# One backbone layer on one core: a gated unit's weights are split in the first loop, its sums lie in three freed banks, and the attention's preparation gets an order

## The chip, the core and the metric

The kernel runs on one core of one Trainium2 chip. The metric is the device time of one execution, in microseconds (us); less is better. The core has five engines that each work through their own list of instructions in order: PE (matrix products into the accumulation banks), DVE, ACT and POOL (elementwise work), and SP (which here only issues transfers). An instruction waits for its inputs, and everything behind it on the same engine waits with it.

## What is computed

One layer of a backbone: an input is normed and modulated, one wide projection feeds three mixers, and the mixers are merged. Only the first part matters here. `h` is the modulated image (1024 tokens by 1024 channels), `hc` the modulated context (256 tokens):

```python
def hybrid_layer(x, xc, c, c_ctx, lp, update_ctx):
    h, gate = modulate(x, c, lp['norm_g'], lp['w_ada'], lp['b_ada'])
    hc, gate_c = modulate(xc, c_ctx, lp['norm_g'], lp['w_ada'], lp['b_ada'])
    z = h @ lp['w_in']
    kc, vc = na_kv(hc @ lp['w_in'][:, A_K:A_Z], lp['k_norm_g'])
    q = na_query(z, lp['q_norm_g'])
    k, v = na_kv(z[..., A_K:A_Z], lp['k_norm_g'])
    ya = neighbourhood_attention(q, k, v, kc, vc, lp['rpb']) * jax.nn.silu(z[..., A_Z:B_B])
    yb = short_conv_branch(z, lp['conv_short_w'])
    yc = conformer_branch(z, lp['conv_conf_w'], lp['conv_conf_b'], lp['ln_conf_g'], lp['ln_conf_b'])
    return x + gate * merge_branches(z, ya, yb, yc, ...)

def conformer_branch(z, w_conv, b_conv, ln_g, ln_b):
    a, g = z[..., C_GLU:C_GLU + D_BRANCH], z[..., C_GLU + D_BRANCH:C_Z]
    u = dw_conv(a * jax.nn.sigmoid(g), w_conv) + b_conv
    ...
```

The "gated unit" is `a * sigmoid(g)`. Its 512 channels are made in four parts of 128, and the first of them (`glu_steps(0, ...)`) is the one the change touches.

## The kernel before

Every product of two numbers in full precision is made of three products of rounded ones: a tensor is split into a high part (a rounded copy) and a low part (the rest), and PE sums high by high, high by low and low by high (`mm3`, lines L107 to L109). So each weight or activation costs a cast (mostly ACT) and a subtraction (DVE or POOL) before PE may use it.

Up to the attention the program does the following.

1. **First loop** (`for k in range(KT)`, eight channel blocks). For each k, `image_ada` makes the modulation of block k on DVE (results A_t, B_t), `modulated` turns four token tiles of x on PE (tile xT_ps), ACT writes the high part `ha` and the full value `xh`, DVE subtracts for the low part (L353). `outer(k, ...)` then adds block k into the query/key/value sums of those four token tiles, all open at once in banks (`first`). `second(k - LAG)` does the same for token tiles 4 and 5 (tiles `hb`), three blocks later. `ctx_ada` (L382, tile `junk`), on DVE, makes the context's modulation out of the same weights: 16 instructions of 1024 columns.
2. **Rest of the image.** `rest_image` modulates token tiles 6 and 7, and `qkv(0, ...)` sums their query/key/value from the finished `h` (L107 to L109, tile ps).
3. **`middle`.** It runs three pieces: first half of the gated unit (weights CGL, sums in tile gps), `context_h` (modulation of the context: tiles `ch`, split with DVE for xh and POOL for the low part), second half of the gated unit (weights CA, sums aps).
4. **Context sums** (`context`, tile psc), then the next head pair's weights (`w1`), then the attention of head pair 0 (`attend(0)`): masks and biases on POOL (L497, L541), `stacks` (copies and splits of q, k, v for one head, L516 to L524), scores (sl, sc), exponent on ACT (L568), and so on. While the attention runs, PE is filled up with the projections of later parts.

Where instructions stand is decided when the program is built: the framework plays the program through on a timeline of its own and gives each engine a fixed list from that. A line moved in the source therefore moves instructions of other lines too. `tc.issue_after(x)` keeps what stands under it behind instruction x in that play, without changing what is computed.

Two pools matter. Banks: there are eight; ps_m has two (tag m), ps_q one (tag q), and pst has tag t (two, for xT_ps) and tag k (three). In the first loop six open sums take m, m, k, k, k, q. Before, both halves of the gated unit take their banks from ps_m, and the context sums take two of the three k banks. Working tiles: rows of 1024 columns (`row4k`, 15 of them) hold x, the ada weights and, before, both weight halves of the gated unit (ghi, glo). The tag `cht` (four tiles) is for the context tiles of later head pairs, which are first loaded in `qkv(1)`.

Of the kernel before, what the change touches and what calls it, by code (L numbers as in the profile page):

```python
# [45 lines left out]
def tile_hybrid(ctx: ExitStack, tc, x, xT, cx, cond, crow, ng, w_ada, b_ada, wqkv, wz,  # L46
# [82 lines left out]

    def qkv(hp, w=None, cts=None, first=(), psc=None, mid=None):  # L130
        w = w or qkv_weights(hp)
# [40 lines left out]
        def context():  # L172
# [3 lines left out]
            vc = [a1.tile([P, 2, P], F32R, tag=f"vc{h}", name="vc") for h in range(2)]  # L176
            pc = psc or [ps_m.tile([P, 512], F32, tag="m", name="psc"), ps_q.tile([P, 512], F32, tag="q", name="psc")]
            for k in range(KT):
# [79 lines left out]

    def glu(i, load=None):
        for _ in glu_steps(i, load):  # L260
            pass

    def glu_steps(i, load=None):
        sg = []
        load = load or (lambda src: load_w(src, KT, pool))
        w = load(wz[CGL + i])
        for b in range(2):
            ps = ps_m.tile([P, 512], F32, tag="m", name="gps")
            mm3(ps, [(w[k][0], w[k][1], hcols(0, k, B512[b]), hcols(1, k, B512[b])) for k in range(KT)])
            t = tmp("flt")  # L270
            act.activation(t, ps, AF.Tanh, scale=0.5)
            sg.append(t)
        yield
        w = load(wz[CA + i])
        for b in range(2):
            ps = ps_m.tile([P, 512], F32, tag="m", name="aps")
            mm3(ps, [(w[k][0], w[k][1], hcols(0, k, B512[b]), hcols(1, k, B512[b])) for k in range(KT)])
            dve.scalar_tensor_tensor(out=sg[b], in0=sg[b], scalar=1.0, in1=ps, op0=ALU.add, op1=ALU.mult)
            nc.sync.dma_start(ud[i][:, B512[b]], sg[b])

    with tc.tile_pool(name="st", bufs=1) as st, tc.tile_pool(name="ps_t", bufs=1, space=PSUM) as pst:
# [107 lines left out]
        def outer(k, ts):  # L389
            for t in ts:  # L390
# [12 lines left out]
        for k in range(KT):  # L403
# [42 lines left out]

        def load_rows(src):
            hi, lo = row4k("ghi", F32R), row4k("glo", F32R)
            for o in range(0, D, 384):
                sl = slice(o, min(o + 384, D))  # L450
                raw = wp.tile([P, 384], F32, tag="wr", name="wr", bufs=3)
                n = sl.stop - o
                state["rows"] = nc.sync.dma_start(raw[:, :n], src[:, sl])
                act.copy(hi[:, sl], raw[:, :n])
                dve.tensor_tensor(out=lo[:, sl], in0=raw[:, :n], in1=hi[:, sl].bitcast(F32), op=ALU.subtract)
            return [(hi[:, k * P : k * P + P], lo[:, k * P : k * P + P]) for k in range(KT)]

        def context_h():
# [7 lines left out]
        def middle():  # L466
            g = glu_steps(0, load_rows)
            for c in (0, 1, 0):
                context_h() if c else next(g, None)
            with tc.issue_after(state["rows"].ins):  # L470
                eight_columns()

        w1raw = []
        for k in range(0, RAW1, 2):
            r = row4k("w1raw")
            nc.sync.dma_start(r[:, :768], wqkv[1, :, k * 384 : k * 384 + 768])
            w1raw += [r[:, :384], r[:, 384:768]]
        qkv(0, w0, ch0, first, [pst.tile([P, 512], F32, tag="k", name="psc", bufs=3) for _ in range(2)], middle)

# [4 lines left out]
    with tc.tile_pool(name="at", bufs=1, reuse_waits="tile") as at, \  # L484
# [10 lines left out]
        for h in range(2):  # L495
            t = at.tile([P, SPAN + 512], F32, name=f"bias{h}")
            pool.memset(t, 1e30)  # L497
            biases.append(t)
        qlz = []
        for h in range(2):  # L500
            t = at.tile([P, QB, P], F32R, name=f"qlz{h}")
            pool.memset(t[HD - h * HD : P - h * HD].bitcast(F32), 0.0)
            qlz.append(t)
# [44 lines left out]
        def scores(b0, qd, ql, ks, kc, bias):  # L548
# [8 lines left out]
            for i in range(2):  # L557
# [9 lines left out]
                dve.tensor_tensor_reduce(pl, sl[:, :n], bias[:, o : o + n], 1.0, mn[:, i : i + 1], ALU.add, ALU.min, mn[:, 2 + i : 3 + i])  # L567
                act.activation(pc, sc[:, i], AF.Exp, bias=mn[:, 2 + i : 3 + i], scale=-1.0, accum_out=mn[:, 4 + i : 5 + i])  # L568
                act.activation(pl, pl, AF.Exp, bias=mn[:, 2 + i : 3 + i], scale=-1.0, accum_out=mn[:, 6 + i : 7 + i])
                pts.append((pt, n))  # L570
            dve.tensor_tensor(out=mn[:, 0:2], in0=mn[:, 4:6], in1=mn[:, 6:8], op=ALU.add)
            dve.reciprocal(out=mn[:, 0:2], in_=mn[:, 0:2])
# [13 lines left out]
        def attend(hp):  # L586
            ya = at.tile([P, 16, 64], F32, tag="ya", name="ya", bufs=1)
            for h in range(2):
                bias = bias_of(2 * hp + h)
                qd, ql, ks, kc, vs, vc = stacks(hp, h)  # L590
                hs = slice(h * HD, h * HD + HD)
# [821 lines left out]
```

## Time and profile before

| | us |
|---|---|
| median of 3 runs (lowest to highest) | 1121.64 (1121.34 to 1122.14) |
| the profiled execution, its own time | 1122.98 |
| its span, first to last instruction | 1121.2 |

| engine | busy us | share of the span |
|---|---|---|
| ACT | 519.8 | 46% |
| POOL | 653.8 | 58% |

An engine's share is a mean over stages that have different limits. Matmuls overlap: a matmul's shown duration is longer than the time to the next one's start, so a count of matmuls times the step between starts tells more than busy time. PEclk is the clock granted to PE, in tenths of full speed. In a timeline row the columns are start (us from the span's start), duration, engine, source line, operation, written tile and read tiles, sizes, count; in square brackets the idle time before it and what ended it.

### The profile page before, as it was taken

Reading aid. Unit: us, or ns where it says so; the run is one execution under the profiler, and the core shown is the slowest. Engines: PE = TensorE matmul, PEld = TensorE weight load, DVE = VectorE, ACT = ScalarE, POOL = GpSimd, SP = SyncE. Lnnn points to the kernel's source line nnn. Section 1 sums busy time; section 2 is a strip of 40 time slices with the busy share of each in tenths; the row PEclk is TensorE's granted clock in tenths of the full one; section 3 lists DMA queues with packets and bytes.
Section 4 is the critical chain, followed back from the end, with each engine's and each line's share of the span. In section 5 each row is a group of like instructions: output and inputs, shape, how many; then the busy total and the mean of one; then the engine's idle time right before and its main releaser. Section 6 shows DMA issues by size and latency. Waiting matters only on the chain. (4 is left out here: it accounts for less than half of the span.)

```text
span 1121.2 us, 15882 instructions
## 1 busy us (share of the span) xinstructions
PE 1084.2 (97%) x5330; PEld 923.2 (82%) x5330; DVE 832.6 (74%) x1368; ACT 519.8 (46%) x1108; POOL 653.8 (58%) x643
## 2 busy tenths in 40 slices
PE   6889999999999999999999999999999999999998
PEld 5768898998998888887888888888888788878766
DVE  6983478666765655557995997897992479879995
ACT  6764576567556554445233232323434434533430
POOL 2254957437636951104958586868777562783860
PEclk7999999999999999999999999999999999999999
DMA  9555414313312332218133424343436996462443
GB/s 351 203 190 190 122 44 120 94 57 93 118 54 85 122 120 70 67 49 326 38 132 104 151 85 160 103 153 139 129 134 237 408 327 222 140 215 66 126 155 122
DMA packets 79458, 163.17 MB, mean 146 GB/s; under 512 B 10289, under 2 KB 31153, under 8 KB 79281
## 3 DMA queue, kind: packets, MB, share of 16 engines
q1 hardware_dynamic: 74768, 160.06, 41.5%
q10 hardware_dynamic: 4608, 2.10, 0.6%
q8 instruction: 42, 0.69, 0.3%
q14 instruction: 40, 0.32, 0.1%
HBM read 120.18 MB, written 44.50 MB: 147 GB/s over the span
## 5 line engine op out<-in xcount | busy, mean ns | idle before, releaser
L751 DVE SCALAR_TENSOR_TENSOR cv<-upad,cf_t,cv 128x512 f32<-128x512 f32 x240 | 166.8, 744 | 0.1
L699 POOL TENSOR_TENSOR wl<-s,wh 128x512 fp32r<-128x512 f32 x69 | 98.4, 1439 | 21.8 <-ACT wh L698 8.1
L90 POOL TENSOR_TENSOR wl<-wr,wh 128x384 fp32r<-128x384 f32 (+1 forms) x57 | 57.3, 1012 | 68.2 <-ACT wh L88 57.6
L698 ACT CAST wh<-s 128x512 fp32r<-128x512 f32 x92 | 55.9, 616 | 87.6 <-POOL s L702 66.0
L584 DVE TENSOR_TENSOR plo<-pp,phi 128x256 fp32r<-128x256 f32 (+2 forms) x96 | 54.5, 576 | 34.8 <-ACT phi L583 34.4
L541 POOL TENSOR_TENSOR bias<-mk,img 64x96 f32<-64x96 bf16 (+1 forms) x96 | 43.7, 462 | 36.9 <-DVE mn L567 20.5
L699 POOL TENSOR_TENSOR wl<-wr,wh 128x512 fp32r<-128x512 f32 x44 | 60.5, 1375 | 4.2 <-ACT wh L698 4.2
L775 PE MATMUL ga<-ha,wh 128*128 128x512 f32 x152 | 59.3, 390 | 1.2 <-ACT wh L698 1.2
L777 PE MATMUL ga<-ha,wl 128*128 128x512 f32 x152 | 59.2, 390 | 0.0
L776 PE MATMUL ga<-ha,wh 128*128 128x512 f32 x152 | 59.2, 390 | 0.0
L583 ACT CAST phi<-pp 128x256 fp32r<-128x256 f32 (+2 forms) x96 | 46.5, 494 | 26.6 <-PE pp L581 25.9
L567 DVE CUSTOM_DVE_ANT_0 pt<-sl,bias,mn 128x384 f32<-128x384 f32 (+1 forms) x64 | 37.2, 581 | 23.0 <-PE sl L564 21.7
L88 ACT CAST wh<-wr 128x384 fp32r<-128x384 f32 (+1 forms) x66 | 31.6, 487 | 39.8 <-PE zaps L108 14.3
L568 ACT ACTIVATE pt<-sc,mn 128x256 f32<-128x256 f32 x64 | 30.4, 475 | 40.1 <-DVE mn L567 40.0
L581 PE MATMUL pp<-ident,pt 128*128 128x128 f32 x304 | 47.0, 273 | 1.6 <-DVE pt L574 1.6
L803 POOL TENSOR_TENSOR s<-wr 128x512 f32<-128x512 f32 x16 | 23.8, 1486 | 38.7 <-DMA wr<-in_wz 38.6
L581 PEld LDWEIGHTS pp<-ident,pt 128*128 128x128 f32 x304 | 37.4, 140 | 9.0 <-ACT phi L583 1.3
L79 POOL TENSOR_TENSOR ssh<-ssh,half_neg 128x4 f32<-128x4 f32 (+1 forms) x40 | 41.4, 1036 | 2.9
L574 DVE TENSOR_SCALAR pt<-pt,mn 128x640 f32<-128x640 f32 (+1 forms) x64 | 41.6, 692 | 0.9
L78 POOL TENSOR_SCALAR ssh<-ssh 128x4 f32<-128x4 f32 (+1 forms) x40 | 10.5, 261 | 53.1 <-DVE ssh L227 49.4
L964 ACT ACTIVATE c<-c 128x512 f32<-128x512 f32 x18 | 11.4, 633 | 63.6 <-DVE c L781 48.0
L109 PE MATMUL ps<-wh,hb 128*128 128x384 f32 x112 | 39.3, 354 | 1.2 <-DVE hb L353 1.1
(421 smaller groups left out, 3896.8 us busy)
## 6 DMA issues: line engine op xcount, KB each, us to landing
wr<-in_wz SPq DMA_DIRECT2D x34, 512.0 KB, 4.0
gs<-gd SPq DMA_DIRECT2D x24, 512.0 KB, 5.0
wada<-in_w_ada SPq DMA_DIRECT2D x16, 512.0 KB, 8.7
wrf<-in_wo SPq DMA_DIRECT2D x16, 512.0 KB, 3.6
wr<-in_wz SPq DMA_DIRECT2D x36, 192.0 KB, 2.4
cht<-chd SPq DMA_DIRECT2D x24, 256.0 KB, 3.1
wro<-in_wout SPq DMA_DIRECT2D x24, 256.0 KB, 5.2
gd<-gate SPq DMA_DIRECT2D x22, 256.0 KB, 4.2
```

Of the source, the lines that this page charges most:

```text
L90: lo_eng.tensor_tensor(out=lo[:, :n], in0=raw[:, :n], in1=hi[:, :n].bitcast(F32), op=ALU.subtract)
L541: pool.tensor_tensor(out=dst, in0=mv, in1=iv, op=ALU.subtract)
L574: dve.tensor_scalar(out=pt[:, SPAN - n :], in0=pt[:, SPAN - n :], scalar1=mn[:, i : i + 1], scalar2=0.5, op0=ALU.mult, op1=ALU.mult)
L581: pe.transpose(out=pp[:, c * P : c * P + P], in_=src, identity=ident)
L583: act.copy(hi, v)
L584: dve.tensor_tensor(out=lo, in0=v, in1=hi.bitcast(F32), op=ALU.subtract)
L698: act.copy(hi, src)
L699: eng.tensor_tensor(out=lo, in0=src, in1=hi.bitcast(F32), op=ALU.subtract)
L751: dve.scalar_tensor_tensor(out=acc[b], in0=src, scalar=cf_t[:, i, j : j + 1], in1=acc[b], op0=ALU.mult, op1=ALU.add)
L775: pe.matmul(ps, wh, bh, start=first and j == 0, stop=False, skip_group_check=True)
L776: pe.matmul(ps, wh, bl, start=False, stop=False, skip_group_check=True)
L777: pe.matmul(ps, wl, bh, start=False, stop=last and j == 3, skip_group_check=True)
```

## The change

Three things change.

- **Weights of the first half.** `load_rows(wz[CGL])` is now called in the first loop, at k = 6 (`GATED`). It splits the 1024 columns in four pieces of 256 (before: 384, 384, 256), into four tiles `grow` of the tag `cht`. The second half (CA) is split as before, in rows, but in pieces of 256.
- **Banks.** The sums gps and aps now use the three banks of tag k, as the image sums that held them are copied out. The context sums go to one bank of ps_m and the bank of ps_q.
- **Order of the attention's preparation.** The four memsets for bias and qlz wait for the last `pow` of the context keys' norm (`state["kc"][0]`). The `stacks` of the second head of pair 0 wait for the first exponent (`state["exp"]`).

```diff
+GATED = 6
-    def qkv(hp, w=None, cts=None, first=(), psc=None, mid=None):
+    def qkv(hp, w=None, cts=None, first=(), mid=None):
...
-            pc = psc or [ps_m.tile([P, 512], F32, tag="m", name="psc"), ps_q.tile([P, 512], F32, tag="q", name="psc")]
+            pc = [ps_m.tile([P, 512], F32, tag="m", name="psc"), ps_q.tile([P, 512], F32, tag="q", name="psc")]
...
-    def glu_steps(i, load=None):
+    def glu_steps(i, load, bank):
...
-            ps = ps_m.tile([P, 512], F32, tag="m", name="gps")
+            ps = bank("gps")
...
-            ps = ps_m.tile([P, 512], F32, tag="m", name="aps")
+            ps = bank("aps")
...
+        gated = []
+
+        def load_rows(src, quarters=None):
+            if quarters:
+                hi, lo = ([t[:, i] for t in quarters[2 * n : 2 * n + 2] for i in range(2)] for n in range(2))
+            else:
+                hi, lo = ([t[:, o : o + 256] for o in range(0, D, 256)] for t in (row4k("ghi", F32R), row4k("glo", F32R)))
+            for o in range(4):
+                raw = wp.tile([P, 384], F32, tag="wr", name="wr", bufs=3)
+                state["rows"] = nc.sync.dma_start(raw[:, :256], src[:, o * 256 : o * 256 + 256])
+                act.copy(hi[o], raw[:, :256])
+                dve.tensor_tensor(out=lo[o], in0=raw[:, :256], in1=hi[o].bitcast(F32), op=ALU.subtract)
...
+            if k == GATED:
+                gated.append(load_rows(wz[CGL], [a1.tile([P, 2, 256], F32R, tag="cht", name="grow", bufs=4) for _ in range(4)]))
...
         def middle():
-            g = glu_steps(0, load_rows)
+            g = glu_steps(0, lambda src: gated.pop() if gated else load_rows(src), lambda name: pst.tile([P, 512], F32, tag="k", name=name, bufs=3))
...
-        qkv(0, w0, ch0, first, [pst.tile([P, 512], F32, tag="k", name="psc", bufs=3) for _ in range(2)], middle)
+        qkv(0, w0, ch0, first, middle)
...
-            pool.memset(t, 1e30)
+            with tc.issue_after(state["kc"][0].ins):
+                pool.memset(t, 1e30)
...
-            pool.memset(t[HD - h * HD : P - h * HD].bitcast(F32), 0.0)
+            with tc.issue_after(state["kc"][0].ins):
+                pool.memset(t[HD - h * HD : P - h * HD].bitcast(F32), 0.0)
...
+            state.setdefault("exp", e)
...
-                qd, ql, ks, kc, vs, vc = stacks(hp, h)
+                with tc.issue_after(state["exp"].ins) if hp == 0 and h else ExitStack():
+                    qd, ql, ks, kc, vs, vc = stacks(hp, h)
```

What this makes of the fixed lists is shown at three places. Most source lines count one more after the change (L107 becomes L108), and buffer numbers differ between the two programs.

PE, end of the first loop, before: tiles hb with a number are channel blocks of the image (669, 683 and 697 are blocks 5, 6 and 7), xT_ps is a turned tile.

```order
L394 MATMUL ps<-wh,hb_641 128x384 x2
L392 MATMUL ps<-wh,hb_669 128x384
L393 MATMUL ps<-wl,hb_669 128x384
L392 MATMUL ps<-wh,hb_669 128x384
L393 MATMUL ps<-wl,hb_669 128x384
L394 MATMUL ps<-wh,hb_669 128x384 x2
L392 MATMUL ps<-wh,hb_683 128x384
L393 MATMUL ps<-wl,hb_683 128x384
L392 MATMUL ps<-wh,hb_683 128x384
L393 MATMUL ps<-wl,hb_683 128x384
L345 MATMUL xT_ps<-ident,xt 128x128 x4
L394 MATMUL ps<-wh,hb_683 128x384 x2
```

PE at the same place now (689 and 703 are blocks 5 and 6); these rows are the end of a run of 20 matmuls gps.

```order
L108 MATMUL gps<-ha_170,grow 128x512
L109 MATMUL gps<-ha_170,grow 128x512
L110 MATMUL gps<-ha_170,grow 128x512
L108 MATMUL gps<-ha_171,grow 128x512
L109 MATMUL gps<-ha_171,grow 128x512
L394 MATMUL ps<-wh,hb_689 128x384 x2
L392 MATMUL ps<-wh,hb_703 128x384
L393 MATMUL ps<-wl,hb_703 128x384
L392 MATMUL ps<-wh,hb_703 128x384
L393 MATMUL ps<-wl,hb_703 128x384
L345 MATMUL xT_ps<-ident,xt 128x128 x3
L394 MATMUL ps<-wh,hb_703 128x384 x2
```

Before, the 48 matmuls gps stood in one run behind all of the image's sums; now 20 stand inside the first loop's last blocks, 4 before the sums of token tiles 6 and 7, and 24 between those.

POOL, from the last context tile to the first bias, before: ch is a context tile, wl the low part of the next pair's weights, ssh the norm's sum of squares, vc the context values.

```order
L353 TENSOR_TENSOR ch_1099<-xh,ch_1099 128x256
L90 TENSOR_TENSOR wl<-wr,wh 128x384
L497 MEMSET bias_1334 128x896
L497 MEMSET bias_1336 128x896
L502 MEMSET qlz_1338 64x1024
L502 MEMSET qlz_1340 64x1024
L78 TENSOR_SCALAR ssh<-ssh 128x2
L90 TENSOR_TENSOR wl<-wr,wh 128x384
L78 TENSOR_SCALAR ssh<-ssh 128x2
L79 TENSOR_TENSOR ssh<-ssh,half_neg 128x2 x2
L209 TENSOR_TENSOR vc<-rawc,vc 128x64 x4
L541 TENSOR_TENSOR bias_1334<-mk,img 64x3x48
```

POOL at the same place now.

```order
L79 TENSOR_SCALAR ssh<-ssh 128x2
L80 TENSOR_TENSOR ssh<-ssh,half_neg 128x2
L91 TENSOR_TENSOR wl<-w1raw,wh 128x384 x3
L91 TENSOR_TENSOR wl<-wr,wh 128x384
L79 TENSOR_SCALAR ssh<-ssh 128x2
L80 TENSOR_TENSOR ssh<-ssh,half_neg 128x2
L210 TENSOR_TENSOR vc<-rawc,vc 128x64 x4
L503 MEMSET bias_1344 128x896
L503 MEMSET bias_1346 128x896
L509 MEMSET qlz_1348 64x1024
L509 MEMSET qlz_1350 64x1024
L548 TENSOR_TENSOR bias_1344<-mk,img 64x3x48
```

The memsets went behind the context values, and three subtractions wl, which before stood between the context tiles, went behind the first norm of the context keys.

SP, the transfers of the same stretch, before: wr is a piece of a weight row, mkd and rpd are the mask and the bias table on their way into another layout, vb is v read back, chd the context tile written out.

```order
L325 DMA xt<-in_cx 128x1024 x2
L476 DMA w1raw<-in_wqkv 128x768 x3
L453 DMA wr<-in_wz 128x384 x2
L453 DMA wr<-in_wz 128x256
L249 DMA mkd<-in_mask 16x2x7680
L250 DMA rpd<-in_rpbs 64x6144
L169 DMA vb<-vd_87 128x1x128 x3
L463 DMA chd<-ch_1051 128x2x512
```

SP at the same place now.

```order
L481 DMA w1raw<-in_wqkv 128x768 x3
L468 DMA chd<-ch_1055 128x2x512
L170 DMA vb<-vd_87 128x1x128 x3
L468 DMA chd<-ch_1071 128x2x512
L170 DMA vb<-vd_87 128x1x128
L405 DMA wr<-in_wz 128x256
L468 DMA chd<-ch_1087 128x2x512
L250 DMA mkd<-in_mask 16x2x7680
L251 DMA rpd<-in_rpbs 64x6144
```

The mask and the bias table now leave behind three of the four context tiles and behind the last weight piece of the second half, which needs a buffer that the first piece frees.

More of the change, by code (lines that the diff above doesn't have):

```diff
@@ L257, in tile_hybrid, with glu @@
     B_t = cst.tile([P, KT, 2], F32, name="B_t")
-    def glu(i, load=None):
-        for _ in glu_steps(i, load):
+    def glu(i):
+        for _ in glu_steps(i, lambda src: load_w(src, KT, pool), lambda name: ps_m.tile([P, 512], F32, tag="m", name=name)):
             pass
-    def glu_steps(i, load=None):
+    def glu_steps(i, load, bank):
         sg = []
-        load = load or (lambda src: load_w(src, KT, pool))
         w = load(wz[CGL + i])
         for b in range(2):
-            ps = ps_m.tile([P, 512], F32, tag="m", name="gps")
+            ps = bank("gps")
             mm3(ps, [(w[k][0], w[k][1], hcols(0, k, B512[b]), hcols(1, k, B512[b])) for k in range(KT)])
@@ L394, in outer @@
                 pe.matmul(o, hcols(1, k, sl), w0[k][0], start=False, stop=k == KT - 1)
+        gated = []
[9 more added lines that the diff above has]
+                dve.tensor_tensor(out=lo[o], in0=raw[:, :256], in1=hi[o].bitcast(F32), op=ALU.subtract)
+            return [(hi[k // 2][:, k % 2 * P : k % 2 * P + P], lo[k // 2][:, k % 2 * P : k % 2 * P + P]) for k in range(KT)]
         hlf.append([])
@@ L445, in tile_hybrid @@
         ch0 = []
[L447 to L456, printed above, removed]
         def context_h():
@@ L567, in scores @@
                 dve.tensor_tensor_reduce(pl, sl[:, :n], bias[:, o : o + n], 1.0, mn[:, i : i + 1], ALU.add, ALU.min, mn[:, 2 + i : 3 + i])
-                act.activation(pc, sc[:, i], AF.Exp, bias=mn[:, 2 + i : 3 + i], scale=-1.0, accum_out=mn[:, 4 + i : 5 + i])
+                e = act.activation(pc, sc[:, i], AF.Exp, bias=mn[:, 2 + i : 3 + i], scale=-1.0, accum_out=mn[:, 4 + i : 5 + i])
                 act.activation(pl, pl, AF.Exp, bias=mn[:, 2 + i : 3 + i], scale=-1.0, accum_out=mn[:, 6 + i : 7 + i])
                 pts.append((pt, n))
+            state.setdefault("exp", e)
             dve.tensor_tensor(out=mn[:, 0:2], in0=mn[:, 4:6], in1=mn[:, 6:8], op=ALU.add)
```

## Prediction

> **What bounds the kernel now.** I read the page first, then stretches of ten microseconds, then the timelines of PE and DVE.
>
> ```profile
> span 1121.2 us, 15882 instructions
> ...
> PE 1084.2 (97%) x5330; PEld 923.2 (82%) x5330; DVE 832.6 (74%) x1368; ACT 519.8 (46%) x1108; POOL 653.8 (58%) x643
> ```
>
> PE is busy for 97% of the span, so a change can save only where PE stands idle or crawls. The stretches show where (PE, its weight loads, DVE, ACT, POOL, each busy us and count; then granted clock, DMA share, GB/s).
>
> ```profile
> 30.00:40.00 10.00, 8.00 (x47) 7.09 (x47) 10.00 (x21) 5.57 (x10) 0.00 (x0) 1.00 1.03 392
> ...
> 60.00:70.00 10.00, 7.13 (x36) 5.06 (x36) 10.00 (x24) 9.10 (x21) 5.54 (x7) 1.00 0.52 154
> 70.00:80.00 10.00, 8.94 (x44) 7.98 (x44) 8.38 (x19) 3.75 (x8) 3.86 (x8) 0.83 0.62 222
> 80.00:90.00 10.00, 10.00 (x46) 8.18 (x45) 2.48 (x6) 2.40 (x5) 3.98 (x6) 1.00 0.45 133
> ...
> 110.00:120.00 10.00, 8.47 (x50) 8.08 (x48) 5.25 (x8) 9.86 (x20) 9.56 (x14) 1.00 0.29 85
> ```
>
> From 30 to 78 DVE has almost no free time and PE waits for it: only 36 matmuls run from 60 to 70. From 80 to 90 it is the reverse: PE is full with the first gated half while DVE works 2.48 of 10. The change lays the second stretch over the first.
>
> How much is lost there? The rows below give the steps between matmul starts, and the ends of two stretches.
>
> ```profile
> 55.38 0.33 PE L392 MATMUL ps<-wh,hb 128*128 128x384 f32 x1
> ...
> 81.12 0.39 PE L107 MATMUL gps<-ha,ghi 128*128 128x512 f32 x1
> ...
> 81.80 0.39 PE L107 MATMUL gps<-ha,ghi 128*128 128x512 f32 x1
> ...
> 90.25 0.60 PE L345 MATMUL xT_ps<-ident,xt 128*128 128x128 f32 x4
> 90.61 0.36 PE L188 MATMUL psc<-wh,ch 128*128 128x256 f32 x1
> ...
> 108.08 0.28 PE L190 MATMUL psc<-wh,ch 128*128 128x256 f32 x1
> ...
> 109.16 0.28 PE L190 MATMUL psc<-wh,ch 128*128 128x256 f32 x1
> 109.28 0.34 PE L107 MATMUL ps<-wh,ha 128*128 128x384 f32 x1
> ...
> 112.92 0.51 PE L107 MATMUL ps<-wh,ha 128*128 128x384 f32 x2
> ...
> 118.58 0.33 PE L198 MATMUL pskc<-ident,tmc 128*128 128x128 f32 x1 [0.44 <-DVE tmc L229]
> 120.00 0.45 PE L107 MATMUL ps<-wh,ha 128*128 128x384 f32 x1 [1.09 <-ACT raw L147]
> ```
>
> A 512-wide matmul steps 0.227 (three in 0.68), a 384-wide one 0.173 (21 in 3.64), a 256-wide one 0.12 (nine in 1.08), a turning one 0.09 (four in 0.36). From 55.38 to 109.28, 53.9 us, the list holds 66 of 384 (11.4), 96 of 512 (21.8), 48 of 256 (5.8) and 48 turns (4.3): 43.3 of work, **10.6 lost**. From 109.28 to 120.00, 10.7 us, it holds 48 of 384, two of 256 and two turns, 8.7: **2.0 lost**, nearly all in the two idle times in brackets. So 12.6 us are there to be had.
>
> Part of the first loss is clock, not idleness:
>
> ```profile
> 71.00:72.00 1.00, 1.00 (x4) 1.00 (x4) 1.00 (x5) 0.34 (x1) 0.28 (x1) 0.50 0.89 344
> ```
>
> After the gaps of 60 to 70 PE ran at half clock. [...]
>
> **The change part by part.**
>
> *Weights split in the first loop.* DVE's rows give the prices.
>
> ```profile
> 65.42 1.35 DVE L455 TENSOR_TENSOR glo<-wr,ghi 128x384 fp32r<-128x384 f32 x3
> ...
> 71.55 0.75 DVE L353 TENSOR_TENSOR hb<-xh,hb 128x256 fp32r<-128x256 f32 x2
> 72.22 0.41 DVE L229 TENSOR_TENSOR tm<-raw,ssh 128x256 f32<-128x256 f32 x1
> ...
> 74.55 0.54 DVE L352 TENSOR_SCALAR xh<-xT_ps,A_t,B_t 128x256 f32<-128x256 f32 x1 [0.44 <-ACT hb L347]
> 75.01 0.41 DVE L229 TENSOR_TENSOR tm<-raw,ssh 128x256 f32<-128x256 f32 x1
> 75.34 1.22 DVE L382 SCALAR_TENSOR_TENSOR junk<-wada,sc 128x1024 bf16<-128x1024 f32 x1
> 76.49 0.42 DVE L353 TENSOR_TENSOR hb<-xh,hb 128x256 fp32r<-128x256 f32 x1
> ...
> 96.41 2.44 DVE L455 TENSOR_TENSOR glo<-wr,ghi 128x384 fp32r<-128x384 f32 x3
> ```
>
> Three pieces took DVE 1.27 (65.42 to the next start). Four of 256 cost 0.335 each, as the two hb at 71.55 do: 1.34. They now stand before DVE's parts for blocks 5 to 7, so PE's stretch starts **1.3 later**. The bounds are 0 (another wait covers them) and 2.4 (the same three pieces beside a busy POOL, at 96.41); I take 1.3, since POOL is idle from 30 to 40. [...]
>
> ACT's four casts lie in its free 4.4 us of 30 to 40; without that cover, 1.3. Three transfers of 128 KB go ahead of the last two ada tiles: at 392 GB/s these come 1.0 later, ahead of DVE's backlog still; without that, 1.0.
>
> *Sums of the first half among the image's.* DVE's last part for token tiles 6 and 7 started at 76.49. Its new list puts ahead of it one more junk (1.24), one more xh (0.46), one more tm (0.34) and 0.07 for the pieces: 78.6, ready at 79.0. PE, starting at 56.7, has 64 of 384, 46 of 512 and about 32 turns before it needs that: 24.4, so it comes at 81.1. DVE is then 2 ahead at the end, where it was behind, and the 10.6 shrink to what is still waited for on the way. Block by block the two lists run within half a microsecond of each other; eight blocks, of which some must miss: **1.0**, bounds 0 and 4.
>
> *What is late next.* The context tiles. ACT now copies two image sums and makes a tanh between them, then come the casts of the second half's weights, and PE's aps wait for the first of these. The list brings PE there at 85.1 without waits (69 of 384, 48 of 512, 14 of 256, 43 turns from 56.7). I put the cost at **1.5**, which is three copies of about 0.5 on ACT, bounds 0 and 6 (the first rival). The second context sum takes the bank of ps_q and waits until the turned keys are copied out:
>
> ```profile
> 77.87 0.33 PE L156 MATMUL psq<-ident,tm 128*128 128x128 f32 x1 [0.78 <-ACT kT L162]
> ```
>
> That wait was 0.78; one matmul covers 0.1 of it: **0.7**, bounds 0 and 1.
>
> *Order of the attention's preparation.* ACT was busy for 9.86 of 110 to 120, with the copies of both heads; the second head's leave, and the 1.09 for `raw` with them. POOL's list holds, behind the first context norm, these:
>
> ```profile
> 109.35 1.01 POOL L90 TENSOR_TENSOR wl<-wr,wh 128x384 fp32r<-128x384 f32 x1 [7.94 <-ACT wh L88]
> 110.30 1.63 POOL L497 MEMSET bias<- 128x896 f32 x2
> 111.99 1.95 POOL L502 MEMSET qlz<- 64x1024 f32 x2
> ...
> 115.58 1.05 POOL L78 TENSOR_SCALAR ssh<-ssh 128x2 f32<-128x2 f32 x1
> 116.71 1.37 POOL L79 TENSOR_TENSOR ssh<-ssh,half_neg 128x2 f32<-128x2 f32 x2
> 118.05 3.17 POOL L209 TENSOR_TENSOR vc<-rawc,vc 128x64 fp32r<-128x64 f32 x4
> 121.19 5.04 POOL L541 TENSOR_TENSOR bias<-mk,img 64x144 f32<-64x144 bf16 x12
> ```
>
> Two norms (at most 1.05 + 0.7 each; I take 1.3), four wl (1.0 each), vc 3.2, memsets 3.6, bias 5.0: 18.4 us in one line, where the memsets had lain in an idle 7.94. The first norm follows the first context sum, which I put near 100.5 (that is 56.7 + 43.8 of work + 3.2 of waits, less 24 matmuls of the second sum): bias at 120, before 126.3. PE has the next pair's sums until then. The matmul with qlz stands inside the third token tile and may wait for its memset: **0.8**, bounds 0 and 3.
>
> *The transfers on SP.* Behind the last weight piece wait the mask, the bias table and, later, the mask's three reads. The mask took 7.4 to land (the longest of the row below) and its reads 3.0.
>
> ```profile
> DMA to landing us min/median/max: 2.8/3.0/7.4
> ```
>
> The mask leaves behind the sixth context tile, near 88.5 (from 79.5 at 0.75 on POOL, two norms and the turns between), and is at hand near 100. ACT asks for it behind the second context sum, near 104: no cost, 4 to spare.
>
> **Sum**, made against the profiled execution (1122.98, span 1121.2): 12.6 lost before; now 1.3 + 1.0 + 1.5 + 0.7 + 0.8 = 5.3; gain 7.3. I take off 0.5 for the rest of the attention, whose list is mixed anew until about 500: **6.8**. That is 1116.2 on the profiled execution; the median of the runs shown is 1.3 lower, so **1114.8**.
>
> **The rivals.**
>
> *The context tiles become the bound.* Before, six of them took from 90.25 until POOL's last part:
>
> ```profile
> 100.66 0.74 POOL L353 TENSOR_TENSOR ch<-xh,ch 128x256 fp32r<-128x256 f32 x1 [0.95 <-DVE xh L352]
> ```
>
> That is 11.1, or 1.85 each. The casts for aps stand behind the seventh. At that pace from 79 they come at 92, and aps start near 92.4 instead of 87.6 (85.1, 1.0 and 1.5): 4.8 to 5 more lost, 1119.8. For it: ACT is in order and gets more between them. Against: those six shared ACT and POOL with the next pair's weights, which are now behind them.
>
> *It does not do what it says:* the sums stand in the list, but PE meets a weight or bank not ready and DVE's turns queue up behind. Then the loss only moves, 1121.6. Against: the list wants them at 57.4 (56.7 and four of 384). The weights' last piece is made by DVE near 50, and the first of the three banks is copied out here, 1.3 later now, at 56.1:
>
> ```profile
> 54.24 0.52 ACT L147 COPY raw<-ps 128x384 f32<-128x384 f32 x1
> ```
>
>
> *Slower.* In the last two head pairs the new list has, among 192 of the attention's matmuls, 289 others, where it had 338: 49 × 0.227 = 11.1 us less cover. If the attention's steps need the old pace, PE idles 11.1 there: 1125.9. It decides where the steps need over 289 × 0.227 = 65.6 us. For it: where cover was thin, PE did wait:
>
> ```profile
> 184.47 0.52 PE L581 MATMUL pp<-ident,pt 128*128 128x128 f32 x3 [1.13 <-DVE pt L574]
> ```
>
> Against: the second pair's 196 had 181 of 384, 96 of 512 and 39 of 256 among them, 58 us, with no longer stall than this and one of 1.1; and PE ends with the same total.
>
> **How the numbers follow.** Forecast 1114.8: 0.72, its own bounds 1110.5 (only the 1.3 and 0.2 of waits: gain 11.1) to 1118.4. Context tiles: 0.13. No effect: 0.06. Slower: 0.09. A measurement of this kernel tells about 0.2%, 2.2 us, from no change. Faster takes the forecast and half of the first rival (0.785), same the other half and the second (0.125), slower the third. Range 1110.5 to 1121.0: it holds the forecast and the first rival, and leaves out no effect, slower and little else.
>
> **What would show it.** In the changed profile 60 to 70 should hold some 45 matmuls at full clock, and no half clock near 71; gps should end near 83, aps start near 87.6, the next pair's sums near 104 (109.28 before) and the third token tile near 112 (120.00). The first bias should be whole near 120. If aps start after 90, the context tiles bound; if the third token tile is early and the end is not, the attention gave it back. I am wrong if DVE shows idle time from 40 to 75, which would mean that PE holds back the turns DVE needs.

## The result, and the profile after

| | before | changed |
|---|---|---|
| median of 9 runs each (lowest to highest), us | 1123.37 (1121.34 to 1124.58) | 1116.53 (1112.81 to 1118.66) |
| the profiled execution, its own time, us | 1122.98 | 1116.31 |

The ratio is 0.9942, with a 95% interval of 0.9928 to 0.9956: about 6.5 us less. Between the two profiled executions it is 6.7 us, where 6.8 were forecast. The median of 1116.53 lies 1.7 above the forecast of 1114.8, since the nine runs of the kernel before lie 1.7 above the three that the forecast was made from (1123.37 and 1121.64).

The page of the changed kernel, span and busy times, then its stretches (PE, weight loads, DVE, ACT, POOL, each busy us and count; granted clock, DMA share, GB/s):

```profile
span 1114.5 us, 15896 instructions
...
PE 1081.2 (97%) x5330; PEld 920.2 (83%) x5330; DVE 827.8 (74%) x1370; ACT 521.7 (47%) x1110; POOL 652.9 (59%) x643
```

```profile
60.00:70.00 10.00, 10.00 (x58) 9.04 (x57) 9.10 (x22) 8.13 (x18) 7.63 (x10) 1.00 0.23 69
70.00:80.00 10.00, 10.00 (x59) 9.15 (x59) 8.42 (x21) 4.13 (x9) 2.97 (x6) 1.00 0.01 2
80.00:90.00 10.00, 8.98 (x55) 7.37 (x54) 6.71 (x13) 6.29 (x15) 6.65 (x11) 1.00 0.41 135
90.00:100.00 10.00, 10.00 (x50) 8.35 (x49) 3.10 (x5) 1.09 (x2) 1.52 (x2) 1.00 0.98 314
```

From 60 to 80 PE is full, 117 matmuls where it ran 80, at full clock (0.83 from 70 to 80 before), while DVE is still nearly full. So the first gated half now lies over DVE's backlog. The spell at half clock is gone with the gaps; that the gaps bring it on was my estimate, from the spell behind 70 in the trace of before, and no run shows how. Before, the clock was 0.68, 0.50, 0.50 and 0.62 in the four microseconds from 70, with PE busy all through; by these shares at most some 1.7 of PE's loss from 55 to 80 was clock (an estimate; at full clock PE might have waited for DVE instead). In the changed kernel:

```profile
71.00:72.00 1.00, 1.00 (x8) 1.00 (x7) 1.00 (x3) 0.05 (x1) 0.92 (x2) 1.00 0.00 0
```

PE's timeline shows where the waits went (start, duration, ..., in brackets the idle time and what ended it):

```profile
55.54 0.62 PE L394 MATMUL ps<-wh,hb 128*128 128x384 f32 x2 [0.70 <-DVE hb L353]
...
56.69 0.39 PE L108 MATMUL gps<-ha,grow 128*128 128x512 f32 x1
...
82.17 0.39 PE L110 MATMUL gps<-hb,grow 128*128 128x512 f32 x1
82.77 0.44 PE L345 MATMUL xT_ps<-ident,xt 128*128 128x128 f32 x2 [0.21 <-DVE xh L352]
...
85.31 0.89 PE L345 MATMUL xT_ps<-ident,xt 128*128 128x128 f32 x4
87.00 0.33 PE L157 MATMUL psq<-ident,tm 128*128 128x128 f32 x1 [0.79 <-DVE tm L230]
...
87.66 0.48 PE L108 MATMUL aps<-ha,ghi 128*128 128x512 f32 x1
...
101.26 0.39 PE L189 MATMUL psc<-wh,ch 128*128 128x256 f32 x1 [0.66 <-ACT kT L163]
...
104.24 0.34 PE L108 MATMUL ps<-wh,ha 128*128 128x384 f32 x1
...
112.95 0.45 PE L108 MATMUL ps<-wh,ha 128*128 128x384 f32 x1
```

The sums of the gated half run from 56.69 to 82.4, aps start at 87.66, the next pair's sums at 104.24, the third token tile at 112.95: 7.05 before its place of 120.00. At the end 6.7 of it are left.

To compare kernels I count each matmul's step to the next start beyond 0.227 (512 wide), 0.174 (384), 0.119 (256) and 0.1 (turn) as PE's loss, by stretches of us, of each kernel's profiled execution:

| kernel | to 55 | 55-80 | 80-105 | 105-120 | 120-140 | 140-350 | behind 350 |
|---|---|---|---|---|---|---|---|
| before | 23.3 | 9.2 | 0.9 | 2.0 | 1.3 | 6.4 | 20.8 |
| changed | 23.8 | 0.8 | 3.2 | 0.7 | 1.5 | 6.6 | 20.8 |
| noord (no order) | 24.1 | 0.9 | 3.2 | 5.7 | 0.7 | 4.7 | 18.3 |
| ordonly (order alone) | 23.4 | 8.7 | 0.9 | 0.0 | 3.5 | 4.3 | 19.7 |
| late (no early weights) | 23.1 | 3.1 | 4.0 | 2.5 | 4.0 | 4.0 | 19.6 |
| nobank (old banks) | 24.6 | 6.7 | 1.0 | 2.1 | 1.5 | 8.5 | 18.6 |
| nomem | 24.1 | 2.3 | 3.2 | 1.3 | 3.0 | 4.9 | 21.9 |
| nostk | 24.3 | 2.2 | 3.2 | 4.9 | 1.5 | 5.3 | 18.3 |
| poollo | 25.3 | 4.5 | 2.3 | 3.5 | 2.6 | 6.0 | 19.9 |
| dbl | 25.7 | 2.6 | 3.3 | 1.0 | 0.9 | 6.3 | 17.4 |
| psck | 23.5 | 1.7 | 2.3 | 4.2 | 1.1 | 5.9 | 19.2 |
| ctxdve | 23.8 | 0.8 | 2.2 | 1.3 | 1.0 | 6.2 | 17.8 |
| cols | 23.8 | 1.7 | 3.8 | 0.0 | 2.7 | 5.8 | 19.7 |

One profile of each kernel stands here, and executions of one kernel lie up to 7 us apart (the changed one's 1112.81 to 1118.66, those of `ctxdve` 1112.27 to 1119.09). Behind 350 the rows spread from 17.4 to 21.9 with no pattern that follows the edits; before and changed agree there, 20.8 each. So a stretch is read for its place, and the whole time from the ratio.

### The profile page after: what moved, and what is told of

The parts are those of the page before. It is cut to its first block, busy times and chain, and to the rows that moved or that the text cites. A ratio compares the mean times of both kernels' runs of the same rounds, so it can differ in the third digit from the quotient of the medians.

```text
span 1114.5 us, 15896 instructions
## 1 busy us (share of the span) xinstructions
PE 1081.2 (97%) x5330; PEld 920.2 (83%) x5330; DVE 827.8 (74%) x1370; ACT 521.7 (47%) x1110; POOL 652.9 (59%) x643
## 5 line engine op out<-in xcount | busy, mean ns | idle before, releaser
L548 POOL TENSOR_TENSOR bias<-mk,img 64x96 f32<-64x96 bf16 (+1 forms) x96 | 45.0, 475 | 24.3 <-DVE mn L574 16.0
L591 ACT CAST phi<-pp 128x256 fp32r<-128x256 f32 (+2 forms) x96 | 46.4, 495 | 23.9 <-PE pp L589 23.3
L812 POOL TENSOR_TENSOR s<-wr 128x512 f32<-128x512 f32 x16 | 23.3, 1455 | 37.1 <-DMA wr<-in_wz 37.1
L89 ACT CAST wh<-wr 128x384 fp32r<-128x384 f32 (+1 forms) x66 | 31.4, 487 | 25.7 <-PE zaps L109 13.0
L108 PE MATMUL ps<-wh,hb 128*128 128x384 f32 x112 | 38.9, 347 | 0.6 <-ACT rawc L197 0.5
```

What stands on the lines that cost most here:

```text
L548: pool.tensor_tensor(out=dst, in0=mv, in1=iv, op=ALU.subtract)
L591: act.copy(hi, v)
```

## The experiments

Each ratio is to the kernel before, run on the same chip; the changed kernel's is 0.9942. The groups of runs had different chips, so kernels are compared by their ratios, and a difference of two ratios is given in us of 1122.

**Which part earns it: four kernels.** `noord` takes the third part away, `ordonly` makes it alone on the kernel before, `late` leaves the early weights out, `nobank` the new banks.

```diff
noord:    -            with tc.issue_after(state["kc"][0].ins):      (both places)
          -                with tc.issue_after(state["exp"].ins) if hp == 0 and h else ExitStack():
ordonly:  these lines, added to the kernel before
late:     -            if k == GATED:
          +            if k == 99:
nobank:   -  lambda name: pst.tile([P, 512], F32, tag="k", name=name, bufs=3))
          +  lambda name: ps_m.tile([P, 512], F32, tag="m", name=name))
          +  pc = [pst.tile(... tag="k" ...) for _ in range(2)] if mid else ...
```

> The change without its third part: early weights and the three banks stay, the four memsets and the second head's stacks are free again. My theory (most of the gain is the first gated half laid over the DVE-bound end of the first loop; the order of the attention's preparation is worth 2.0 - 0.8 = 1.2 us): about 1.2 us above the changed kernel, 1117.5 to 1118.5 where the changed one has 1116.5, ratio to before 0.995 to 0.996; aps start near 87.7 as in the changed kernel, and the 1.09 us wait of PE for raw is back before the third token tile. Rival (the order part earns the larger share): 1121 or more, ratio 0.998 or more.

> Before with the third part alone: memsets behind the context keys' norm, second head's stacks behind the first exponent; weights and banks as before. My theory: PE's 10.6 us of loss from 55 to 109 are untouched, the 2.0 behind them shrink to 0 to 0.8: 1.2 to 2.0 us below before, ratio 0.998 to 0.999. Rival (the order part earns the larger share): 4 us or more below, ratio 0.996 or less. Second rival (the attention's list, mixed anew, decides): anything up to 2 us above before, with the difference behind 130 us.

> The change with its weights split late again (after the image, in rows, pieces of 256), banks and order as changed: the list may lay gps over the image's last part, but only from where DVE has made the low parts, near 66. The losses before were 2.9 us from 55 to 65 and 6.3 from 65 to 80. My theory as the prediction has it names the early weights and the banks together; by the loss alone, what lies in front of 66 cannot be filled (2.9 less the 1.3 that the early splits cost): 1.5 to 2 us above the changed kernel, ratio 0.995 to 0.997. Rival A (the early weights are the cause): nearly all of the first part is lost, 5 us or more above the changed kernel, ratio 0.998 or more. Rival B (the banks alone are the cause): as the changed kernel within 0.5 us, ratio 0.994 to 0.9945.

> The change with the old banks: weights split early into the context tiles' places and order as changed, but gps and aps in the two banks of ps_m, context sums in two k banks. The list then has gps behind the image's sums as before, since both m banks belong to the image until then. My theory: the first loop's end keeps its loss of about 10 us, and DVE's 1.3 is only moved; what is left is the order part: 1121 to 1122.5, ratio 0.998 to 0.9995, with 36 to 42 matmuls from 60 to 70 and a half clock near 71. Rival (early weights relieve DVE by themselves: its three low parts at 65.42 are gone): 2 to 4 us below before, ratio 0.9965 to 0.998.

| | noord | ordonly | late | nobank |
|---|---|---|---|---|
| ratio | 0.9971 | 0.9976 | 0.9983 | 1.0003 |
| 95% interval | 0.9960 to 0.9983 | 0.9967 to 0.9985 | 0.9974 to 0.9992 | 0.9992 to 1.0013 |
| median, us (before: 1122.08) | 1119.04 | 1119.52 | 1119.77 | 1121.86 |

The order alone gives 2.7 us (0.0024 of 1122), and without it the change gives 3.3: the shares are near equal, and 0.9971 times 0.9976 is 0.9947, the changed kernel's ratio within its interval. I had expected 1.2 for the order. In the profile of `ordonly` the 2.0 from 105 to 120 are gone, but 2.2 more are lost from 120 to 140: its 2.7 is a whole time, and only the 2.0 have a place. `noord`'s trace shows what it is worth once the sums come earlier. PE, then ACT, then POOL of `noord`:

```profile
113.83 0.39 PE L568 MATMUL sl<-ks,qd 128*128 128x256 f32 x1 [1.10 <-DVE ks L527]
...
114.83 0.33 PE L199 MATMUL pskc<-ident,tmc 128*128 128x128 f32 x1 [0.50 <-DVE tmc L230]
117.56 0.44 PE L108 MATMUL ps<-wh,ha 128*128 128x384 f32 x1 [2.40 <-ACT raw L148]
```

```profile
112.91 1.04 ACT L521 CAST qd<-qT 64x1024 fp32r<-64x1024 f32 x1
...
116.09 0.62 ACT L528 CAST vs<-vb 128x512 fp32r<-128x512 f32 x1
...
117.03 0.85 ACT L148 COPY raw<-ps 128x384 f32<-128x384 f32 x2
```

```profile
108.95 1.63 POOL L502 MEMSET bias<- 128x896 f32 x2
110.64 1.95 POOL L507 MEMSET qlz<- 64x1024 f32 x2
112.57 1.77 POOL L80 TENSOR_TENSOR ssh<-ssh,half_neg 128x2 f32<-128x2 f32 x1
```

The second head's casts (four, 112.91 to 116.6) stand ahead of the copy `raw`, which frees a bank for the third token tile: PE waits 2.40, not 1.09. The memsets stand ahead of the norm that tmc needs. With the sums early, PE's work came forward by some 5 us (the next pair's sums from 109.28 to 104.24 in the changed kernel), and ACT's and POOL's lists did not follow. From 105 to 120 `noord` loses 5.7, which is 5.0 more than the changed kernel; the expectations below name that difference.

`late` and `nobank` say that of the first two parts neither works without the other: both have the order too, and neither is faster than the order alone. With the new banks but late weights PE starts the gated half at 63.73 and loses 3.1 from 55 to 80, but then it waits for the context tiles (1.23 at 85.22, and 2.10 at 133.09 for the transfer of one that the next pair needs): it is no faster than `ordonly`. So the loss only moves, as in the prediction's second rival, but not for its reason: PE waits for context tiles, not for a weight or a bank of the gated half. With early weights but old banks the sums do not start before 77.59, as in the list, and the four splits are paid for nothing: 3.0 slower than `ordonly`, no gain left, and a little worse than the 0.998 to 0.9995 expected. The splits account for 1.1 to 1.9 of the 3.0 (worked out under "Why the prediction was right"); the rest has no cause shown. The kernels that keep the gaps keep the slow spell: the mean granted clock is 0.83 from 60 to 70 in `ordonly`, and 0.90 and 0.93 in the two tens from 60 in `nobank`, where 384-wide matmuls step 0.32 instead of 0.174 (67.10 to 68.70 in `ordonly`, 68.17 to 70.09 in `nobank`). `late` has 1.00 from 60 to 80, and in `noord` one 384-wide matmul follows another there in 0.17 to 0.19. `late` is 4.6 above the changed kernel, where I had expected 1.5 to 2; that counted the hole but not what came behind it. Its ratio is the one that rival A gave: without the early weights nearly all that the first two parts earn is lost.

```profile
63.73 0.50 PE L108 MATMUL gps<-ha,ghi 128*128 128x512 f32 x1
...
85.22 0.38 PE L189 MATMUL psc<-wh,ch 128*128 128x256 f32 x1 [1.23 <-ACT ch L347]
...
133.09 0.39 PE L189 MATMUL psc<-wh,cht 128*128 128x256 f32 x1 [2.10 <-DMA cht<-chd]
```

```profile
77.59 0.48 PE L108 MATMUL gps<-ha,grow 128*128 128x512 f32 x1
```

(The first three rows are PE of `late`, the last PE of `nobank`.)

**The two halves of the order.** `nomem` frees the memsets alone, `nostk` the second head's stacks alone.

> The change with the four memsets free again; only the second head's stacks wait. The kernel without both lost 5.0 us from 105 to 120 (0.7 in the changed one): PE waited 1.10 for ks, 0.50 for tmc, 2.40 for raw, and ACT had the second head's four casts (3.75 us) ahead of raw. My theory: the stacks are what counts, so here 105 to 120 lose 0.7 to 1.7 (the 0.50 for tmc behind the memsets, and what they delay), and the time is 0 to 1 us above the changed kernel: ratio to before 0.994 to 0.9955. Rival (the memsets in front of POOL's second norm are what counts): 3 us or more lost there, ratio 0.9965 or more.

> The change with the second head's stacks free again; only the memsets wait. My theory: the wait of PE for raw of 2.4 us or more is back between 112 and 120, with ACT's casts of both heads ahead of raw; 105 to 120 lose 3 to 4.5, and the time is 2 to 3.5 us above the changed kernel: ratio to before 0.996 to 0.9975. Rival (the memsets are what counts): within 1 us of the changed kernel, ratio 0.994 to 0.9955.

Measured: `nomem` 0.9955 (0.9940 to 0.9971), `nostk` 0.9958 (0.9943 to 0.9973). The places came nearly as expected: without the stacks' wait PE waits 2.88 for raw and loses 4.9 from 105 to 120 (3 to 4.5 expected); without the memsets' it loses 1.3 there. The totals did not separate, and `nostk` came out below the 0.996 to 0.9975 of my theory. `nomem` loses 3.0 from 120 to 140 instead of 1.5, and `nostk` less behind 140. Each alone costs 1.5 to 1.8 us by its ratio, and both intervals overlap the changed kernel's, so only the two together (`noord`) are certain.

```profile
119.04 0.44 PE L108 MATMUL ps<-wh,ha 128*128 128x384 f32 x1 [2.88 <-ACT raw L148]
```

**The term of 1.3 us.** `poollo` lets POOL make the four low parts; `dbl` has DVE make them twice.

```diff
poollo: -                dve.tensor_tensor(out=lo[o], in0=raw[:, :256], ...)
        +                (pool if quarters else dve).tensor_tensor(out=lo[o], in0=raw[:, :256], ...)
dbl:    +                if quarters:
        +                    dve.tensor_tensor(out=lo[o], in0=raw[:, :256], ...)
```

> The change with the four low parts of the early weights subtracted on POOL instead of DVE; POOL stood idle for 18.57 us up to 42.41. It tests the term of 1.3 us (four splits of 0.335 on a DVE without free time). Theory (the 1.3 was paid): PE's stretch of gps starts near 55.4 instead of 56.7, and 1.3 us are gained against the changed kernel: 1115.0 to 1115.5 where it has 1116.5, ratio to before 0.993. Rival A (another wait covers it): as the changed kernel within 0.3, ratio 0.994 to 0.9945. Rival B (POOL's reads slow DVE's two-input instructions in the same time): DVE loses 0.4 or more for each of the four, and the gain shrinks to 0 or turns into up to 1 us of loss.

> The change with each of the four early subtractions made twice on DVE, one behind the other: it doubles the term of 1.3 us. Theory (DVE has no free time until gps, so every split ahead of the parts of blocks 5 to 7 starts PE's full stretch later): gps start 1.3 later than in the changed kernel (58.0 instead of 56.7), PE's loss up to 80 us 1.3 higher (25.9 instead of 24.6), and 1 to 1.5 us more in the end: ratio to before 0.995 to 0.9955. Rival (the splits lie under other waits, of ACT above all, or the gain in the first loop comes back later): within 0.3 of the changed kernel, ratio 0.994 to 0.9945.

`dbl`: 0.9963 (0.9951 to 0.9975), 2.4 us above the changed kernel, though the two intervals overlap a little. The sums start 2.1 later than in the changed kernel's profile, and DVE's parts miss PE again at 72.62. PE, then DVE of `dbl`:

```profile
58.80 0.39 PE L108 MATMUL gps<-ha,grow 128*128 128x512 f32 x1
...
72.62 0.44 PE L110 MATMUL ps<-wh,hb 128*128 128x384 f32 x1 [1.27 <-DVE hb L353]
```

```profile
56.41 0.76 DVE L337 TENSOR_SCALAR xt<-xt,pad 128x1024 f32<-128x1024 f32 x1 [0.71 <-POOL pad L80]
```

Not all of the 2.1 is the doubling. DVE's first early split starts at 38.72 in `dbl` and at 38.02 in the changed kernel, with the same list up to there, so 0.7 is a difference between two executions, and 1.4 is added behind it, near the 1.3 of the theory. That 1.4 also holds the wait of 0.71 for a norm of POOL, which the changed kernel's profile does not have, less one `junk` that the list now has later. So the cost is real and is not given back; that a microsecond on DVE costs PE just one is not shown. `poollo`: 0.9983 (0.9973 to 0.9992), 4.6 us above the changed kernel: not the gain of 1.3 but a loss well beyond rival B's. POOL, then DVE of `poollo`, then DVE of the changed kernel:

```profile
35.71 2.51 POOL L407 TENSOR_TENSOR grow<-wr,grow 128x256 fp32r<-128x256 f32 x2 [11.55 <-ACT grow L406]
41.52 1.55 POOL L407 TENSOR_TENSOR grow<-wr,grow 128x256 fp32r<-128x256 f32 x1 [3.31 <-ACT grow L406]
```

```profile
36.67 0.95 DVE L353 TENSOR_TENSOR hb<-xh,hb 128x256 fp32r<-128x256 f32 x1
37.55 1.75 DVE L373 SCALAR_TENSOR_TENSOR junk<-wada,sc 128x1024 bf16<-128x1024 f32 x1
...
41.25 1.22 DVE L373 SCALAR_TENSOR_TENSOR junk<-wada,sc 128x1024 bf16<-128x1024 f32 x1
...
42.40 1.22 DVE L353 TENSOR_TENSOR ha<-xh,ha 128x512 fp32r<-128x512 f32 x1
```

```profile
36.35 0.42 DVE L353 TENSOR_TENSOR hb<-xh,hb 128x256 fp32r<-128x256 f32 x1
36.69 1.22 DVE L373 SCALAR_TENSOR_TENSOR junk<-wada,sc 128x1024 bf16<-128x1024 f32 x1
...
41.90 0.69 DVE L353 TENSOR_TENSOR ha<-xh,ha 128x512 fp32r<-128x512 f32 x1
```

Each POOL split held up one DVE instruction by 0.53 (the fourth, at 50.77, held a wl: 1.07 for 0.55), so four cost DVE 2.1 to save 1.3. The rows show that the hold goes both ways. With DVE out of its way POOL took 0.74 for a subtraction of 128x256 (the row at 100.66 in the prediction); here the first two took 2.51 together, the third 1.55 and the fourth 1.63. The first, third and fourth began while DVE was in a `junk` (35.53 to 36.75, 41.25 to 42.47, 50.61 to 51.81). The third began at 41.52, DVE's `junk` ended at 42.47, POOL ended 0.60 behind that, at 43.07, and DVE's ha, begun at 42.40, ended 0.55 behind POOL. So by these rows POOL's 1.55 holds a wait of its own, and DVE's 0.53 lies in what was left of POOL's subtraction (42.47 to 43.07).

DVE's net loss of 0.8 (2.1 less 1.3) is what the start of the sums shows: DVE was 0.32 late already at 35.53 (35.21 in the changed kernel), the sums start 1.15 late (57.84), so 0.83 is added between. It leaves 3.8 of the 4.6. In the profile PE waits further for DVE's hb, 1.38 at 70.56 and 0.86 at 74.31, and for ks 1.52 at 119.28, none of which the changed kernel has; that these are the 3.8, and why DVE is late there, is not shown. The lists of ACT and DVE near 55 were mixed anew too.

**The terms behind the gated half.** `psck` gives the second context sum a k bank instead of ps_q's; `ctxdve` lets DVE instead of POOL make the context's low parts.

```diff
psck:   +  pc = [ps_m.tile(... "psc"), pst.tile(... tag="k", name="psc", bufs=3) if mid else ps_q.tile(... "psc")]
ctxdve: -                    modulated(k + i, xc, 1, c[:, i, :L], c[:, i, L:], dve, pool)
        +                    modulated(k + i, xc, 1, c[:, i, :L], c[:, i, L:], dve, dve)
```

> The change with the second context sum of the first head pair in a k bank (as an aps sum frees it) instead of the bank of ps_q. It tests the term of 0.7 us (PE waits 0.66 at 101.26 until the turned keys are copied out of ps_q's bank). Theory: that wait goes, nothing takes its place: 0.5 to 0.7 below the changed kernel, ratio to before 0.9935 to 0.994. Rival A (the third k bank comes free only when DVE has read the first aps, which now ends later; the wait is for DVE instead): no change, ratio 0.994 to 0.9945. Rival B (the attention's list, mixed anew, decides): a difference behind 120 us of 1 us or more to either side.

> The change with the low parts of the context tiles subtracted on DVE instead of POOL. From 80 to 105 PE lost 3.2 us in the changed kernel, most of it between the context tiles (0.21 for xh, a row of four turns that took 0.89, 0.79 for tm, whose norm stands on POOL between the low parts). The prediction's term was 1.5 for ACT alone. Theory (the chain over POOL holds the turns and tm): aps start 0.5 to 1.0 earlier than 87.66, 0.5 to 1 us gained, ratio to before 0.993 to 0.994. Rival (ACT's copies and casts set that pace): aps start within 0.2, no change, ratio 0.994 to 0.9945.

`psck`: 0.9940 (0.9922 to 0.9958), no different. The wait of 0.66 is gone, and PE comes earlier to the first score, where ks is not ready. It waits there instead, and loses 4.2 from 105 to 120 (PE of `psck`):

```profile
113.75 0.36 PE L570 MATMUL sl<-ks,qd 128*128 128x256 f32 x1 [1.41 <-DVE ks L529]
```

`ctxdve`: 0.9941 (0.9924 to 0.9957), no difference that can be told, though PE's loss from 80 to 105 falls from 3.2 to 2.2 and aps start at 87.16, 0.5 earlier. Its DVE, then that of the changed kernel:

```profile
86.53 0.42 DVE L230 TENSOR_TENSOR tm<-raw,ssh 128x256 f32<-128x256 f32 x1
...
87.77 0.75 DVE L407 TENSOR_TENSOR glo<-wr,ghi 128x256 fp32r<-128x256 f32 x2
```

```profile
86.00 0.94 DVE L230 TENSOR_TENSOR tm<-raw,ssh 128x256 f32<-128x256 f32 x1
...
87.77 2.17 DVE L407 TENSOR_TENSOR glo<-wr,ghi 128x256 fp32r<-128x256 f32 x3
```

The same hold again: beside POOL's low parts tm took 0.94 and three glo 2.17; without POOL tm took 0.42 and two glo 0.75.

**The transfers.** `cols` issues the mask's and the bias table's copies behind the next pair's first weights, near 60; `colsctx` does so on top of `ctxdve`.

```diff
-            with tc.issue_after(state["rows"].ins):
+            with tc.issue_after(state["w1r"].ins):
                 eight_columns()
```

> The change with the mask's and the bias table's transfers behind the next pair's first weights instead of behind the second gated half's weights. In the changed kernel they left at 90.25 and 90.92 and took 8.2 and 11.8 us, the DMA engines were busy for 0.98 of 90 to 100, and every transfer of that time took 9 to 12 us; from 70 to 80 they were busy for 0.01. Theory A (that jam is covered: nothing of PE waits for it in the changed kernel, the mask is cast at 107.18 and the biases hang on POOL): transfers behind 90 take 2 to 4 us again, the time stays within 0.7 of the changed kernel, ratio 0.9935 to 0.9945. Theory B (the jam delays the next pair's weights on ACT, which waited 1.20 for them at 105.36, and with them the attention's start): 1 to 2 us gained, ratio 0.9925 to 0.9935.

> Both edits together: context low parts on DVE, and the mask's and bias table's transfers in the stretch from 59 on, in which the DMA engines were idle. If both theories of gain hold they add: 1.5 to 2.5 us below the changed kernel, ratio to before 0.992 to 0.993, and this is the faster version. If neither holds: 0.994 to 0.9945. If the attention's list, mixed anew, decides: 1 us or more to either side, with the difference behind 110 us.

The DMA issues from 88 to 104 (KB each, median us to landing), of the changed kernel and of `cols`:

```profile
rpd<-in_rpbs SPq DMA_DIRECT2D x1, 1536.0 KB, 11.8
...
wr<-in_wqkv SPq DMA_DIRECT2D x2, 192.0 KB, 8.3
vb<-vd SPq DMA_DIRECT2D x5, 64.0 KB, 10.0
```

```profile
vb<-vd SPq DMA_DIRECT2D x6, 64.0 KB, 2.8
...
wr<-in_wqkv SPq DMA_DIRECT2D x2, 192.0 KB, 3.1
```

The jam is gone, and 105 to 120 lose 0.0, but the ratio is 0.9957 (0.9945 to 0.9969): no gain, and by its middle 1.7 us worse. 80 to 105 lose 0.6 more and 120 to 140 lose 1.2 more, the latter in waits for context tiles. `colsctx` is at 0.9948 (0.9935 to 0.9961). So ending the jam is not shown to gain anything, as theory A said, though both ratios lie above the range it gave, and no version tried here is shown to beat the changed kernel.

## Why the prediction was right

*What was to be had, 12.6.* Right: the third token tile came 7.05 earlier, and that is the 12.1 that I count with the steps above, less some 5 that are still lost (5.3 forecast).

*1.3 for the early splits.* Right in size, with a second part that I had not seen. The row of two matmuls that first wait for hb behind 54 stands at 54.92, 54.98 and 54.69 without early splits (before, ordonly, late; mean 54.86), and at 55.54 to 56.99 in the nine kernels with them on DVE once (mean 56.26): 1.4. DVE's lists are the same up to the first split, and there the profiles already lie up to 0.9 apart (38.02 in the changed kernel to 38.93). Counted from that place to DVE's work on `xt` (L337; 53.78 before, 54.41 now), five of the nine took 1.08 more than the three without early splits, and the other four (`nobank`, `nomem`, `nostk`, `colsctx`) 1.87, with a wait of 0.71 for a norm of POOL; there ACT had waited 0.40 to 0.49 for a transfer of x. So the splits are 1.1, and in some executions a late transfer adds 0.8. The profiled changed kernel is one of the five and the earliest at the first split: 0.6 to the eye, and gps at 56.69 where I had 57.4.

*1.0 for block-by-block waits.* Right: from 56.69 to 82.17 PE lost 0.8. The ten microseconds from 60 hold 58 matmuls, not the 45 I named; PE lost 0.5 in them, and even with all of the 1.0 there it would have run over 50, so the sign was set too low.

*1.5 for the context tiles.* The time was right (aps at 87.66, forecast 87.6), the size and the reason only partly. From 82.17 to 87.66 PE lost 2.1: 0.21 for xh, 0.3 in the row of four turns (0.89, elsewhere 0.60), 0.79 for tm and the rest in small steps. None of it is the wait for the first ghi that I priced: gps ended 0.6 earlier than forecast (82.4 for 83), and the tiles cost 0.6 more than the 1.5, which is luck. The tm was slow beside POOL's low parts, as `ctxdve` shows. The first rival (aps behind 90) did not come.

*0.7 for ps_q's bank.* Right to the place: 0.66 at 101.26. `psck` adds that removing it gains nothing, since ks is late next.

*0.8 for qlz, and the transfers' 4 to spare.* The first was not paid: the memset ended near 114.8, the matmul stood at 116.19. The second was too easy. POOL, ACT and PE, and SP's issues, of the changed kernel:

```profile
112.86 1.95 POOL L509 MEMSET qlz<- 64x1024 f32 x2
114.78 4.65 POOL L548 TENSOR_TENSOR bias<-mk,img 64x144 f32<-64x144 bf16 x12
```

```profile
107.18 0.43 ACT L497 CAST mk<-mt__1335 128x288 bf16<-128x288 f32 x1
```

```profile
116.19 0.28 PE L571 MATMUL sl<-ks,qlz 128*128 128x256 f32 x1
```

```profile
90.92 0.58 SPq L251 DMA_DIRECT2D rpd<-in_rpbs  x1
102.73 0.33 SPq L496 DMA_DIRECT2D mt__1335<-mkd  x1
```

The first bias was whole at 119.4 (forecast 120), but by two errors: POOL's line began with the norm at 102.22 where I had 100.5 and took 17.2 where I had 18.4. My own figures do not give the 120 either: 56.7 + 43.8 + 3.2 less 2.9 is 100.8, and with 18.4 it is 119.2. But the mask's reads left only when the bias table's copy of 11.8 us was through (SP waited 3.8 for it): I had given the mask 7.4 and left that second copy out. The reads do not need that copy's data: in `cols` the same read left at 68.08, when the mask had landed (59.75 and 8.3), with the bias table's copy still under way until 71.6. So the wait of 3.8 is not for the data; what else holds the read is not shown. The first of the reads landed near 106.2, 1 us before ACT's cast. No cost of it is shown (`cols`).

*The order of the preparation, 2.0 less 0.8.* The term that was most mis-sized. I priced its wait at the 1.09 of the trace before. With PE 5 us earlier the wait for raw is 2.40 to 2.88 (`noord`, `nostk`), and the order is worth about 3 us. The rest of the change by itself is worth 3.3, not the 5.6 that 6.8 less 1.2 leaves for it: some of what it saves it loses again at once at 112 to 118. The sum did not need this split, since it counted the waits behind 109 as gone with both made together; so the total is right and the shares are not.

*The attention, 0.5, and the slower rival.* From 112.95 to the end 0.4 was given back. The feared thin cover of the last two head pairs did not cost: from 350 to 510 PE lost 4.3 before and 4.0 now, the largest wait being 0.96, for pt at 365.33.

*The sum.* Against 1.3 + 1.0 + 1.5 + 0.7 + 0.8 = 5.3 stand, in this profile, 0.6 (1.1 without the early start) + 0.8 + 2.1 + 0.7 + 0 = 4.2 to 4.7. The mechanism is the one forecast, but that the whole came within 0.3 is luck in part: the context tiles were 0.6 too cheap and the qlz matmul 0.8 too dear, and executions of one kernel differ by far more than that.

*What would have made it wrong.* I named idle DVE time between 40 and 75. There was one of 0.90, at 63.76, but it hung on POOL's norm and not on PE's turns:

```profile
63.76 0.42 DVE L230 TENSOR_TENSOR tm<-raw,ssh 128x256 f32<-128x256 f32 x1 [0.90 <-POOL ssh L80]
```

## What to carry to other kernels

Work to fill an engine's hole needs its data and its bank at the same time; with one of the two the hole stayed or moved, and the preparation was paid for nothing (PE's loss from 55 to 80 was 0.8 with both, 6.7 with the data alone, 3.1 with the banks alone). When a change brings one engine forward, price the waits behind it at their new place: the other engines' lists are still where they were, and a wait of 1.09 became 2.40. Before moving work from a full engine to an idle one, check in a trace whether the idle one, once it works, holds up the full one's next instructions (in `poollo` by 0.52 to 0.53 us each).

## What was not expected of the hardware

A POOL subtraction of 128x256 held one DVE instruction (`hb`, `junk`, `ha`, `wl`) by 0.52 to 0.53 us (0.42 to 0.95, 1.22 to 1.75, 0.69 to 1.22, 0.55 to 1.07) and was itself held by the DVE instruction before (2.51 for two, 1.55 and 1.63, where one took 0.74 before), so 1.3 us of work taken off DVE cost it 2.1. The transfers that SP issued behind the bias table's copy from memory to memory landed behind it: they took 7 to 12 us, where the medians of `vb`, `wr` and `chd` from 88 to 104 were 2.8, 3.1 and 3.4 in `cols`, with that copy 30 us earlier.
